# Halving the first and last quarter of the modulated input: two modulation vectors loaded, and w_in applied, in six parts instead of four

## Chip, cores and metric

One core of a Trainium2 chip. The metric is the device time of one execution in microseconds (us); of the kernel before, three runs gave a median of 1733.25 us (1733.23 to 1736.04).

## What is computed

A block of a streaming encoder over 256 positions of width 2048, in f32. What the change touches is its beginning:

```python
mod  = silu(c) @ w_ada + b_ada                  # six vectors of 2048
sh_m, sc_m, gt_m, sh_f, sc_f, gt_f = split(mod, 6)
h    = rms_norm(x, g_norm_mix) * (1 + sc_m) + sh_m
proj = h @ w_in          # 1024 columns of q and kv latent, 64 of rotary key, 3 x 1024 of the convolution
```

Then come the convolution and the attention on `proj`, `w_out`, a second modulated norm, and PEER: the 128 x 128 experts' scores against all keys, the best 16 per head, and the sum over the chosen rows of `peer_v`.

## The kernel before

Everything is held transposed: features on the 128 partitions, the 256 positions on the free axis, in 16 blocks of 128 features. A matrix product in f32 is made of three: each operand is split into a high and a low half (high = rounded copy by ScalarE, low = rest by VectorE, L198 and L199 for weights, L366 and L367 for h), and TensorE adds high x high, high x low and low x high (in column block 0 the low weights come second). A matmul of that kind has 128 x 128 weights and 256 columns.

The first two modulation vectors (m = 1, the scale, and m = 0, the shift) are made in quarters, 512 features each, by `ada_q(q)`. A quarter of a vector is 4 MB of `w_ada`, in four **chunks** of 1 MB (L407, buffers `t8`, six of them). Some chunks are multiplied by TensorE (L411: the activated c as weights in four column groups of 32, four matmuls of 512 columns a chunk, into `adarow`), by `ADA_PE` two of four for the scale and three of four for the shift; the rest by VectorE (L415, L417: four accumulating steps a chunk into `acc`). L420 adds both, the **column sums** (L423: four matmuls with one column) turn the row into columns, L316 adds the bias into `modc`. For the scale, L431 then makes x * rstd * (1 + scale) (`xs`); for the shift, `shift_split` makes the high and low half of h from it.

With a quarter of h the first 12 column blocks of `w_in` are worked on, in `unit`: 12 units, each of 4 feature blocks x 3 products = 12 matmuls (L694) into six PSUM tiles `pin` that stay open over all quarters. Their weights lie in `w_in0`, 12 tiles of 1 MB: three tiles per quarter, each with 4 column blocks x 4 feature blocks. A weight tile has a raw buffer (4 of them) and a high and a low buffer (2 of each), so the split of a tile waits until the tile two before it has been read.

Between the units the generator of the next quarter's modulation is advanced by the table `UNITS` (unit number: steps). A scheduler then orders the instructions of each engine; they run strictly in that order. All these loads are issued by the one queue of SyncE, in order. After each third of the last quarter's units, `after_in0` copies finished latent rows out (L681), and `lat_chain` squares and sums them (L474 to L480), takes the sum over features on TensorE (`ssl`, L341), the inverse root (L346 to L352, four small VectorE steps and a root on ScalarE) and spreads it by a matmul (`rlb`, L358). Then `conv_group` and `proj` go on with the other `w_in` tiles (`pwin`, L213, L214, L217).

Of the kernel before, what the change touches and what calls it, by code (L numbers as in the profile page):

```python
# [15 lines left out]
ALU = mybir.AluOpType  # L16
# [42 lines left out]
ADA_LAST = (0, 0, 1)  # L59
ADA_PE3 = (2, 5, 8, 11, 14)  # L60
PACES = {"start": 1.0, "latent": 1.15, "mixer": 1.35, "out": 0.83}
ADA_PE = {1: (1, 3), 0: (1, 2, 3)}
UNITS = {1: 1, 2: 1, 3: 1, 4: 1, 6: 1, 7: 1, 8: 2, 9: 1, 10: 1}
ABLK = 8
TB = 16

# [66 lines left out]
def hybrid_block_kernel(  # L133
# [22 lines left out]
    nc = tc.nc  # L156
# [81 lines left out]
    with tc.tile_pool(name="pre", bufs=1) as pre:  # L238
# [159 lines left out]
        xsv = {}  # L398

        def ada_q(q):  # L400
            for m in (1, 0):
                acc = s2(f"acc{m}_{q}")
                prow = ps_tile(f"adarow{m}_{q}")
                on_pe = ADA_PE[m]
                for kg in range(4):
                    raw = t8(f"ada{m}_{q}_{kg}", shape=(128, 4, 512))
                    nc.sync.dma_start(raw.rearrange("p a b -> p (a b)"), w_ada01[q, 1 - m, kg])  # L407
                    for j in range(4):
                        k = 4 * kg + j
# [12 lines left out]
                for j in range(4):  # L422
                    PE.matmul(prow[:, j:j + 1], lhsT=acc[:, j * 128:(j + 1) * 128], rhs=ones[:, 0:1],  # L423
                              start=True, stop=True)
                ada_cols(m, 4 * q, prow[:, :4])
                if m == 1:
                    xs = s2(f"xs{q}a"), s2(f"xs{q}b")
                    xsv[q] = [x_.rearrange("p (c t) -> p c t", c=2) for x_ in xs]
                    for j in range(4):
                        c = 4 * q + j  # L430
                        V.scalar_tensor_tensor(xsv[q][j // 2][:, j % 2], xt[:, c], modc[:, 1, c:c + 1], r0,  # L431
                                               ALU.mult, ALU.mult)
                yield

        def tiles():
# [252 lines left out]
        def unit(q, g, n, w):  # L688
            whi, wlo = w
            dst = pin[2 * g + n // 2][:, (n % 2) * 256:(n % 2) * 256 + 256]  # L690
            first = q == 0 and n % 2 == 0

            def one(j, wt, ht, start=False, stop=False):
                PE.matmul(dst, lhsT=wt[:, (4 * n + j) * 128:(4 * n + j + 1) * 128], rhs=ht[:, 4 * q + j],  # L694
                          start=start, stop=stop, skip_group_check=True)

            if g == 0 and n == 0:
                for j in range(4):
                    one(j, whi, h[0], first and j == 0)
                for j in range(4):  # L700
                    one(j, wlo, h[0])
                for j in range(4):
                    one(j, whi, h[1], False, q == 3 and j == 3)
                return
            for j in range(4):
                one(j, whi, h[0], first and j == 0)
                one(j, whi, h[1])
            for j in range(4):
                one(j, wlo, h[0], False, q == 3 and j == 3)

        def take0(i):
            return load_split(w_in0[i % NG0, i // NG0], f"win0_{i % NG0}_{i // NG0}", 0)

        for _ in ada_q(0):
            pass
        ws0 = {0: take0(0)}
        for q in range(4):
            nxt = ada_q(q + 1) if q < 3 else ada
            for j in range(4):
                c = 4 * q + j  # L720
                shift_split(xsv[q][j // 2][:, j % 2], modc[:, 0, c:c + 1], h[0][:, c], h[1][:, c])
            for u in range(4 * NG0):
                g, n = divmod(u, 4)
                i = NG0 * q + g
                if n == 0 and i + 1 < 4 * NG0:
                    ws0[i + 1] = take0(i + 1)
                unit(q, g, n, ws0[i])
                if q < 3:
                    for _ in range(UNITS.get(u, 0)):
                        next(nxt, None)  # L730
                elif n == 3:
                    after_in0(g)
                    for _ in range(ADA_LAST[g]):
                        next(nxt, None)
            if q == 0:
# [769 lines left out]
```

## Time and profile before

| | |
|---|---|
| median of three runs | 1733.25 us |
| the profiled execution | 1736.56 us, its span 1734.8 us |
| TensorE matmuls busy | 1671.4 us (96%) |
| VectorE busy | 1138.4 us (66%) |
| ScalarE busy | 704.6 us (41%) |
| DMA, mean over the span | 292 GB/s |

Spans and starts are in us from the start of the profiled execution. A granted clock of 1.00 is 2.4 GHz, 0.50 is 1.2 GHz. TensorE's matmuls overlap: a row's duration reaches to the modelled end, so the pace is read from the starts of consecutive rows. A matmul in f32 appears as two records (x8 for a chunk of four).

### The profile page before, as it was taken

The page shows a single profiled execution, that of the slowest core. Times are in us where ns is not written, and L with a number is a line of the kernel's source. Part 1 is how long each engine was busy: PE and PEld are TensorE (multiplying, and loading weights), DVE is VectorE, ACT ScalarE, POOL GpSimd, SP SyncE. Part 2 cuts the span into 40 slices and gives each one's busy share as a digit, 9 for nine tenths or more (in the row PEclk, how much of TensorE's full clock was granted, in tenths as well). Part 3 has the DMA queues.
Part 4 walks back from the last instruction along what each step waited for, and adds up shares of the span by engine and source line. Part 5 has one row for each costly group of instructions (what it writes and reads, how often), then busy time and mean ns, then how long its engine had stood idle before and what let it go on. Part 6 is the DMA issues. An engine that isn't in the chain of part 4 may idle for free. (4 is left out here: it accounts for less than half of the span.)

```text
span 1734.8 us, 30084 instructions
## 1 busy us (share of the span) xinstructions
PE 1671.4 (96%) x13011; PEld 1437.9 (83%) x13011; DVE 1138.4 (66%) x1481; ACT 704.6 (41%) x783; POOL 300.7 (17%) x257
## 2 busy tenths in 40 slices
PE   4999999999899999999999999999999999999996
PEld 2879899899899999999998999999999654444542
DVE  5778778767668989998985788765644332322324
ACT  3225557434544446645653343334343232222312
POOL 0000000000000000000001000000021486777771
PEclk9989999999999999999999999999999999999998
DMA  9987888878654456646678887879888699999895
GB/s 395 425 366 266 329 315 330 309 274 339 239 198 169 170 198 206 247 172 220 230 245 296 310 304 245 300 271 324 311 337 309 226 398 395 343 381 352 323 386 212
DMA packets 77928, 505.95 MB, mean 292 GB/s; under 512 B 9472, under 2 KB 10112, under 8 KB 22496
## 3 DMA queue, kind: packets, MB, share of 16 engines
q1 hardware_dynamic: 44784, 319.82, 49.1%
q0 software_dynamic: 29712, 162.94, 25.6%
q10 hardware_dynamic: 3296, 21.24, 3.2%
q8 instruction: 103, 1.69, 0.4%
q14 instruction: 33, 0.27, 0.0%
HBM read 466.21 MB, written 37.75 MB: 291 GB/s over the span
## 5 line engine op out<-in xcount | busy, mean ns | idle before, releaser
L213 PE MATMUL pu<-h2hi,hu 128*128 128x256 f32 x2048 | 495.3, 284 | 0.0
L198 ACT ACTIVATE hu<-ru 128x2048 fp32r<-128x2048 f32 x128 | 245.5, 1918 | 423.0 <-PE pu L214 382.6
L199 DVE TENSOR_TENSOR lu<-ru,hu 128x2048 fp32r<-128x2048 f32 x128 | 293.0, 2289 | 165.9 <-ACT hu L198 162.4
L213 PEld LDWEIGHTS pu<-h2hi,hu 128*128 128x128 f32 x2048 | 386.8, 189 | 0.2 <-issue 0.2
L217 PE MATMUL pu<-h2hi,lu 128*128 128x256 f32 x2048 | 264.5, 282 | 4.3 <-DVE lu L199 4.3
L217 PEld LDWEIGHTS pu<-h2hi,lu 128*128 128x128 f32 x2048 | 252.9, 190 | 4.5 <-DVE lu L199 4.5
L214 PE MATMUL pu<-h2loT3b,hu 128*128 128x256 f32 x1024 | 248.1, 281 | 0.0
L214 PE MATMUL pu<-h2loT3a,hu 128*128 128x256 f32 x1024 | 248.1, 281 | 0.0
L1293 PE MATMUL po<-rv,mc 128*64 128x512 f32 (+2 forms) x1064 | 221.7, 597 | 5.0 <-DMA mc<-actd,perm_idx 3.1
L214 PEld LDWEIGHTS pu<-h2loT3a,hu 128*128 128x128 f32 x1024 | 193.7, 189 | 0.2 <-issue 0.2
L214 PEld LDWEIGHTS pu<-h2loT3b,hu 128*128 128x128 f32 x1024 | 193.4, 189 | 0.0
L1293 PEld LDWEIGHTS po<-rv,mc 128*64 128x64 f32 (+2 forms) x1064 | 70.1, 130 | 145.5 <-issue 136.2
L1190 POOL DMA_DIRECT2D gg<-gd x16 | 18.8, 1172 | 905.3 <-DMA gd<-stage 905.3
L1242 POOL DMA_INDIRECT mc<-actd,perm_idx x109 | 134.8, 1237 | 36.8 <-issue 29.9
L1235 POOL DMA_INDIRECT rv<-in_peer_v_dram,perm_idx x107 | 129.2, 1207 | 61.5 <-issue 28.6
L204 DVE TENSOR_TENSOR lv<-rv,hv 128x2048 fp32r<-128x2048 f32 x24 | 55.0, 2293 | 115.4 <-ACT hv L203 115.3
L203 ACT ACTIVATE hv<-rv 128x2048 fp32r<-128x2048 f32 x24 | 45.9, 1914 | 123.4 <-DMA rv<-in_peer_v_dram,perm_idx 110.1
L199 DVE TENSOR_TENSOR lwin<-rwin,hwin 128x2048 fp32r<-128x2048 f32 x33 | 75.6, 2290 | 24.6 <-ACT hwin L198 24.5
L198 ACT ACTIVATE hwin<-rwin 128x2048 fp32r<-128x2048 f32 x33 | 63.1, 1913 | 61.0 <-PE pin L694 32.1
L204 DVE TENSOR_TENSOR third<-rv,third 128x2048 fp32r<-128x2048 f32 x12 | 27.6, 2296 | 89.4 <-ACT third L203 89.4
L1201 POOL DMA_DIRECT2D actd<-A x16 | 14.9, 934 | 407.0 <-DVE A L1196 224.3
L213 PE MATMUL pwin<-hhi,hwin 128*128 128x256 f32 x336 | 82.9, 289 | 0.0
(534 smaller groups left out, 2932.1 us busy)
## 6 DMA issues: line engine op xcount, KB each, us to landing
ru<-in_peer_u_dram SPq DMA_DIRECT2D x128, 1024.0 KB, 6.1
ada<-in_w_ada_dram SPq DMA_DIRECT2D x96, 1024.0 KB, 7.0
rwin<-in_w_in_dram SPq DMA_DIRECT2D x33, 1024.0 KB, 6.5
rwout<-in_w_out_dram SPq DMA_DIRECT2D x16, 1024.0 KB, 5.3
rwq<-in_w_q_dram SPq DMA_DIRECT2D x16, 1024.0 KB, 4.9
gd<-stage ACTq DMA_DIRECT2D x16, 1024.0 KB, 6.0
gg<-gd POOLq DMA_DIRECT2D x16, 1024.0 KB, 11.5
actd<-A POOLq DMA_DIRECT2D x15, 1024.0 KB, 6.3
```

Of the source, the lines that this page charges most:

```text
L198: S.activation(hi, raw, AF.Copy)
L199: V.tensor_tensor(lo, raw, hi.bitcast(F32), ALU.subtract)
L203: S.activation(hi, src, AF.Copy)
L204: V.tensor_tensor(lo, src, hi.bitcast(F32), ALU.subtract)
L213: PE.matmul(dst, lhsT=whi[:, sl], rhs=rhi[:, c], start=(c == sets[0][0]), stop=False)
L214: PE.matmul(dst, lhsT=whi[:, sl], rhs=rlo[:, c], start=False, stop=False)
L217: PE.matmul(dst, lhsT=wlo[:, sl], rhs=rhi[:, c], start=False, stop=(c == sets[-1][-1]))
L1190: keep(nc.gpsimd.dma_start(gg, gd[:, :, k * ABLK:(k + 1) * ABLK, :].rearrange("tb p i t -> p tb i t")))
L1201: keep(nc.gpsimd.dma_start(actd[k * ABLK * 128:(k * ABLK + n) * 128].rearrange("(i p) t -> p i t", p=128), ab[k][:, :n]))
L1235: keep(nc.gpsimd.indirect_dma_start(raw, None, v_rows, index(main[n])))
L1242: keep(nc.gpsimd.indirect_dma_start(ms[-1][:, n % 8], None, actd[:, :], index(main[n])))
L1293: keep(PE.matmul(po[tt * 4 + d4][row:row + size], lhsT=m[:, at * size:(at + 1) * size], rhs=raw[:, d4 * 512:(d4 + 1) * 512], start=start, ...
```

## The change

The first and the last quarter are each handled as two halves of 256 features, so that there are six parts: 0a, 0b, 1, 2, 3a, 3b. A half's modulation is made by `ada_half`: two chunks per vector, each with 8 feature blocks x 256 columns, and all of them go to TensorE, 8 matmuls of 256 columns a chunk; L455 masks the sum, and two column sums follow. Quarters 1 and 2 still use `ada_q`. The units of a half have 6 matmuls. In the halved quarters the three weight tiles are laid out anew: the first holds the first half's blocks 0 to 7, the second its blocks 8 to 11 and the second half's 0 to 3, the third the second half's 4 to 11.

```diff
-UNITS = {1: 1, 2: 1, 3: 1, 4: 1, 6: 1, 7: 1, 8: 2, 9: 1, 10: 1}
+UNITS = ({1: 1, 2: 1, 3: 1, 4: 1, 6: 1, 7: 1, 8: 2, 9: 1, 10: 1}, {1: 1, 3: 1, 4: 1, 6: 1, 8: 1, 9: 1})
+HALVED = (0, 3)
+PIECES = tuple((4 * q + 2 * k, 4 - 2 * (q in HALVED)) for q in range(4) for k in range(1 + (q in HALVED)))
+HALF0 = ([(0, n) for n in range(8)], [(0, n) for n in range(8, 12)] + [(1, n) for n in range(4)],
+         [(1, n) for n in range(4, 12)])
...
+        def ada_half(q, half):
+            for m in (1, 0):
+                prow = ps_tile(f"adarow{m}_{q}h{half}")
+                acc = s2(f"acc{m}_{q}h{half}")[:, :256]
+                for kg in range(2):
+                    raw = t8(f"ada{m}_{q}h{half}_{kg}", shape=(128, 8, 256))
+                    nc.sync.dma_start(raw.rearrange("p a b -> p (a b)"), w_ada01[q, 1 - m, 2 * half + kg])
+                    for j in range(8):
+                        k, r = 8 * kg + j, 32 * (j % 4)
+                        PE.matmul(prow[r:r + 32, :256], lhsT=cact[:, k:k + 1].to_broadcast([128, 32]), rhs=raw[:, j],
+                                  start=(k < 4), stop=(k >= 12), tile_position=(0, r))
+                    if kg == 0:
+                        yield
+                V.tensor_scalar(acc, prow[:, :256], quad, None, ALU.mult)
+                yield
+                for j in range(2):
+                    PE.matmul(prow[:, j:j + 1], lhsT=acc[:, j * 128:(j + 1) * 128], rhs=ones[:, 0:1],
+                              start=True, stop=True)
+                ada_cols(m, 4 * q + 2 * half, prow[:, :2])
+                if m == 1:
+                    scale_x(4 * q + 2 * half, 2)
                 yield
...
-        for q in range(4):
-            nxt = ada_q(q + 1) if q < 3 else ada
...
+        for q, (c0, size) in enumerate(PIECES):
+            nxt = ada_piece(q + 1) if q < end0 else ada
+            for c in range(c0, c0 + size):
+                shift_split(xsv[c // 2][:, c % 2], modc[:, 0, c:c + 1], h[0][:, c], h[1][:, c])
+            for u, (i, n, off) in enumerate(work0[q]):
+                if i + 1 < 4 * NG0 and i + 1 not in ws0:
                     ws0[i + 1] = take0(i + 1)
-                unit(q, g, n, ws0[i])
-                if q < 3:
-                    for _ in range(UNITS.get(u, 0)):
+                unit(n, range(c0, c0 + size), ws0[i], off, n == 0)
+                if q < end0:
+                    for _ in range(UNITS[PIECES[q + 1][1] == 2].get(u, 0)):
                         next(nxt, None)
```

On TensorE, at the border to quarter 1, the order was, with `adarow_1_420` the shift's row (the scale's, `adarow_1_303`, stands among the units well before):

```order
L694 MATMUL pin_181<-hhi,lwin_2_0_349 128x256 x2
L411 MATMUL adarow_1_420<-ada_1_3_469,cact 32x512 x4
L694 MATMUL pin_181<-hhi,lwin_2_0_349 128x256 x2
L423 MATMUL adarow_1_420<-ones,acc_1_419 128x1 x4
L694 MATMUL pin_176<-hhi,hwin_0_1_429 128x256
```

and of the change, where `adarow_1_413` is the scale's row and `adarow_1_494` the shift's, it is:

```order
L729 MATMUL pin_181<-hhi,lwin_2_0_352 128x256 x2
L415 MATMUL adarow_1_413<-ada_1_3_456,cact 32x512 x4
L427 MATMUL adarow_1_413<-ones,acc_1_412 128x1 x4
L415 MATMUL adarow_1_494<-ada_1_1_507,cact 32x512 x4
L415 MATMUL adarow_1_494<-ada_1_2_513,cact 32x512 x4
L415 MATMUL adarow_1_494<-ada_1_3_525,cact 32x512 x4
L427 MATMUL adarow_1_494<-ones,acc_1_493 128x1 x4
L729 MATMUL pin_176<-hhi,hwin_0_1_446 128x256
```

The scale's last chunk and its sums, and all of the shift's chunks, now stand between the units of part 0b and those of part 1.

On VectorE, at the end of the last part, the order before was (`lwin_1225` is the first weight tile behind the twelve, `rl0r` and `rl0v` the root's steps, `lacc` the sums of squares):

```order
L346 TENSOR_SCALAR rl0v<-ssl_1118 128x2
L199 TENSOR_TENSOR lwin_1225<-rwin_1222,hwin_1224 128x2048
L349 RECIPROCAL rl0r<-rl0r 128x2
L479 TENSOR_TENSOR lacc_1132<-lsq_1131 128x256
L350 SCALAR_TENSOR_TENSOR rl0v<-rl0v,rl0r 128x2
L500 TENSOR_TENSOR krT<-kraw,rope_t 128x256
L351 TENSOR_TENSOR rl0v<-rl0v,rl0r 128x2
L480 TENSOR_TENSOR lacc_1132<-lacc_1132 128x256
L352 SCALAR_TENSOR_TENSOR rl0r<-rl0v,rl0r 128x2
```

and of the change, where `lwin_1307` is the first weight tile behind the twelve and `lwin_1313` the second, it is:

```order
L203 TENSOR_TENSOR lwin_1307<-rwin_1304,hwin_1306 128x2048
L509 TENSOR_TENSOR lacc_1194<-lsq_1193 128x256
L507 TENSOR_TENSOR lacc_1238<-lsq_1237 128x256
L510 TENSOR_TENSOR lacc_1194<-lacc_1194 128x256
L530 TENSOR_TENSOR krT<-kraw,rope_t 128x256
L350 TENSOR_SCALAR rl0v<-ssl_1224 128x2
...
L203 TENSOR_TENSOR lwin_1313<-rwin_1310,hwin_1312 128x2048
L353 RECIPROCAL rl0r<-rl0r 128x2
...
L356 SCALAR_TENSOR_TENSOR rl0r<-rl0v,rl0r 128x2
```

The split that stands before the root's last steps is now that of the second tile, no longer that of the first. On TensorE the broadcast `rlb` that needs `rl0r` stands, in both, right behind the last unit and before the first matmul of `pwin`.

On TensorE the first units of part 0a read, in the change (`hwin_0_0` and `lwin_0_0` are the first tile's high and low half):

```order
L458 MATMUL adarow_0h_217<-ones,acc_0h_218 128x1 x2
L729 MATMUL pin_176<-hhi,hwin_0_0_245 128x256 x2
L729 MATMUL pin_176<-hhi,lwin_0_0_246 128x256 x2
L729 MATMUL pin_176<-hlo,hwin_0_0_245 128x256 x2
L729 MATMUL pin_176<-hhi,hwin_0_0_245 128x256
```

The low half of the weights is read by the third matmul; before, eleven matmuls stood ahead of the first one that reads it. On SyncE's queue the second and third weight tile of the last quarter (`rwin_1_3`, `rwin_2_3`), which followed the last modulation chunk, now stand before it. Behind this stage the order of every engine is the same as before but for a few neighbours that change places.

## Rows read from the trace of the kernel before

**Rows 1.** Busy time by stretches: engines' busy us, clock, DMA share, GB/s.
```profile
core 0: us, PE busy (x) PEld busy (x) DVE busy (x) ACT busy (x) POOL busy (x), PEclk, DMA share, GB/s
37.70:44.50 6.80, 4.88 (x23) 4.88 (x24) 5.49 (x6) 4.07 (x4) 0.00 (x0) 0.50 1.01 425
44.50:68.40 23.90, 22.67 (x180) 17.47 (x179) 16.46 (x24) 4.45 (x4) 0.00 (x0) 1.00 1.01 423
68.40:71.80 3.40, 3.40 (x16) 3.40 (x17) 2.08 (x5) 2.88 (x4) 0.00 (x0) 0.50 1.03 436
123.00:129.90 6.90, 6.11 (x29) 6.02 (x29) 4.14 (x6) 3.51 (x5) 0.00 (x0) 0.51 0.32 134
```

**Rows 2.** Timeline of TensorE (PE): start us, duration us, line, operation, count.
```profile
21.49 1.22 PE L358 MATMUL n0b<-ident,n0r 128*128 128x128 f32 x4 [3.55 <-DVE n0r L352]
22.64 3.64 PE L411 MATMUL adarow<-ada,cact 128*32 128x512 f32 x16
39.62 0.58 PE L694 MATMUL pin<-hhi,hwin 128*128 128x256 f32 x1 [3.39 <-ACT hwin L198]
47.67 1.06 PE L411 MATMUL adarow<-ada,cact 128*32 128x512 f32 x8
48.66 0.39 PE L694 MATMUL pin<-hhi,hwin 128*128 128x256 f32 x1
55.48 1.06 PE L411 MATMUL adarow<-ada,cact 128*32 128x512 f32 x8
57.42 1.05 PE L423 MATMUL adarow<-ones,acc 128*128 128x1 f32 x8
62.81 0.63 PE L694 MATMUL pin<-hhi,lwin 128*128 128x256 f32 x4
63.28 0.28 PE L694 MATMUL pin<-hhi,hwin 128*128 128x256 f32 x1
64.55 1.06 PE L411 MATMUL adarow<-ada,cact 128*32 128x512 f32 x8
66.49 1.05 PE L423 MATMUL adarow<-ones,acc 128*128 128x1 f32 x8 [0.44 <-DVE acc L420]
68.33 0.98 PE L694 MATMUL pin<-hhi,hwin 128*128 128x256 f32 x3 [0.80 <-ACT hhi L366]
95.87 1.01 PE L694 MATMUL pin<-hhi,hwin 128*128 128x256 f32 x3 [0.79 <-ACT hhi L366]
117.81 2.78 PE L411 MATMUL adarow<-ada,cact 128*32 128x512 f32 x24
144.18 0.61 PE L358 MATMUL rlb<-ident,rl0r 128*128 128x128 f32 x4
144.99 0.36 PE L213 MATMUL pwin<-hhi,hwin 128*128 128x256 f32 x1
```

**Rows 3.** Issues of modulation chunks, 105.4 to 105.6 us, with their time to landing.
```profile
L407 SPq DMA_DIRECT2D ada<-in_w_ada_dram x2: 327/371/415, 105.1 to 105.5; - x2
DMA to landing us min/median/max: 8.4/9.4/10.4
```

**Rows 4.** Waits of TensorE from 160 us to the end, longest group: total, times, longest.
```profile
PE pu L217 <- DVE lu L199: 4.3, 1, 4.3
```

**Rows 5.** Timeline of VectorE (DVE).
```profile
7.90 6.24 DVE L376 TENSOR_TENSOR sacc<-sacc,xsq 128x256 f32<-128x256 f32 x12
36.27 0.16 DVE L316 TENSOR_TENSOR modc<-adarow,vec 128x4 f32<-128x4 f32 x1 [1.14 <-PE adarow L423]
60.50 0.48 DVE L415 TENSOR_SCALAR acc<-ada,cact 128x512 f32<-128x512 f32 x1
61.01 2.33 DVE L417 SCALAR_TENSOR_TENSOR acc<-ada,cact,acc 128x512 f32<-128x512 f32 x3
139.74 2.29 DVE L199 TENSOR_TENSOR lwin<-rwin,hwin 128x2048 fp32r<-128x2048 f32 x1 [0.97 <-ACT hwin L198]
143.15 0.15 DVE L352 SCALAR_TENSOR_TENSOR rl0r<-rl0v,rl0r 128x2 f32<-128x2 f32 x1
```

**Rows 6.** Timeline of ScalarE (ACT), the weight split before the end of the stage.
```profile
137.79 1.92 ACT L198 ACTIVATE hwin<-rwin 128x2048 fp32r<-128x2048 f32 x1 [1.10 <-PE pin L694]
```

More of the change, by code (lines that the diff above doesn't have):

```diff
@@ L426, in ada_q, with scale_x @@
                 if m == 1:
[L427 to L432, printed above, removed]
+                    scale_x(4 * q, 4)
+                yield
+        def scale_x(c0, n):
+            for c in range(c0, c0 + n, 2):
+                x_ = s2(f"xs{c}")
+                xsv[c // 2] = x_.rearrange("p (c t) -> p c t", c=2)
+                for j in range(2):
+                    V.scalar_tensor_tensor(xsv[c // 2][:, j], xt[:, c + j], modc[:, 1, c + j:c + j + 1], r0,
+                                           ALU.mult, ALU.mult)
+        def ada_half(q, half):
[12 more added lines that the diff above has]
+                V.tensor_scalar(acc, prow[:, :256], quad, None, ALU.mult)
+                yield
+                for j in range(2):
+                    PE.matmul(prow[:, j:j + 1], lhsT=acc[:, j * 128:(j + 1) * 128], rhs=ones[:, 0:1],
[3 more added lines that the diff above has]
+                    scale_x(4 * q + 2 * half, 2)
                 yield
@@ L686, in after_in0, with unit @@
                 spawn(rope(krT, kraw[:, :256], "kr", kr_place))
-        def unit(q, g, n, w):
+        def unit(n, cs, w, off, tail=False):
             whi, wlo = w
[L690 to L709, printed above, removed]
+            dst = pin_nt(n)
+            first = cs[0] == 0 and n % 2 == 0
+            last = cs[-1] == 15
+            hh = [(whi, h[0], c) for c in cs]
+            hl = [(whi, h[1], c) for c in cs]
+            lh = [(wlo, h[0], c) for c in cs]
+            ops = hh + lh + hl if tail else [x for y in zip(hh, hl) for x in y] + lh
+            for k, (wt, ht, c) in enumerate(ops):
+                o = off + (c - cs[0]) * 128
+                PE.matmul(dst, lhsT=wt[:, o:o + 128], rhs=ht[:, c], start=first and k == 0,
+                          stop=last and k == len(ops) - 1, skip_group_check=True)
@@ L711, in take0, with ada_piece @@
         def take0(i):
             return load_split(w_in0[i % NG0, i // NG0], f"win0_{i % NG0}_{i // NG0}", 0)
-        for _ in ada_q(0):
+        def ada_piece(k):
+            q, half = divmod(PIECES[k][0], 4)
+            return ada_half(q, half // 2) if q in HALVED else ada_q(q)
+        work0 = []
+        for c0, size in PIECES:
+            q, half = divmod(c0, 4)
+            if q in HALVED:
+                work0.append([(NG0 * q + g, n, 256 * k) for g, us in enumerate(HALF0) for k, (p, n) in enumerate(us)
+                              if 2 * p == half])
+            else:
+                work0.append([(NG0 * q + n // 4, n, (n % 4) * 512) for n in range(4 * NG0)])
@@ L715, in hybrid_block_kernel @@
+        end0 = len(PIECES) - 1
+        for _ in ada_piece(0):
             pass
         ws0 = {0: take0(0)}
-        for q in range(4):
-            nxt = ada_q(q + 1) if q < 3 else ada
[L719 to L725, printed above, removed]
+        for q, (c0, size) in enumerate(PIECES):
[4 more added lines that the diff above has]
+                if i + 1 < 4 * NG0 and i + 1 not in ws0:
@@ L726, in hybrid_block_kernel @@
                     ws0[i + 1] = take0(i + 1)
-                unit(q, g, n, ws0[i])
-                if q < 3:
-                    for _ in range(UNITS.get(u, 0)):
+                unit(n, range(c0, c0 + size), ws0[i], off, n == 0)
+                if q < end0:
+                    for _ in range(UNITS[PIECES[q + 1][1] == 2].get(u, 0)):
                         next(nxt, None)
-                elif n == 3:
-                    after_in0(g)
-                    for _ in range(ADA_LAST[g]):
+                elif n % 4 == 3:
+                    after_in0(n // 4)
+                    for _ in range(ADA_LAST[n // 4]):
@@ L734, in hybrid_block_kernel @@
                         next(nxt, None)
+            if q < end0:
+                for _ in nxt:
+                    pass
             if q == 0:
@@ L1465 @@
     ada01 = np.ascontiguousarray(ada01).reshape(4, 2, 4, 128, 2048)
+    for q in HALVED:
+        part = w_ada[:, :, 1::-1, 512 * q:512 * q + 512].reshape(2, 8, 128, 2, 2, 256).transpose(3, 4, 0, 2, 1, 5)
+        ada01[q] = part.reshape(2, 4, 128, 2048)
     w_ada = w_ada[:, :, 2:].transpose(2, 0, 1, 3)
```

5 lines of the change are left out of this document (4 added, 1 removed).

## Prediction

> **What bounds the kernel now.** I read the busy time by stretches first, cut where the granted clock changes [rows 1]. In the stretch from 44.5 to 68.4 us two things are full at once: the DMA engines (share 1.01, 423 GB/s) and TensorE (22.67 of 23.90 us). Which of them ends the stage is told by TensorE's own order [rows 2]: a run of 4 unit matmuls takes 0.47 us (62.81 to 63.28), 0.1175 each, and 144 of them make 16.9 us. A loaded chunk of 1 MB on TensorE takes 1.0 us (47.67 to 48.66), and some 0.2 go at the two changes of form between it and the units around it (the matmul behind it takes 0.39, not 0.28): 1.2 us in the midst of units. A set of column sums is 1.05. From the first unit at 39.62 to the last, whose follower starts at 144.18, I count 576 x 0.1175 = 67.7 us of units, 15 chunks, 6 sets of column sums, gaps at the three borders between quarters, and stretches at the lower of the clock's two levels, 1.2 GHz instead of 2.4. Three of these stand in rows 1: 6.8 us from 37.7, 3.4 us from 68.4 and 6.9 us from 123; each begins at a gap before new units, and in the one of 3.4 us there is room for 16 matmuls where 29 would fit. So TensorE is the chain. The last modulation chunk is issued at 105.5 and lands 10.4 us later, at 115.9 [rows 3], but TensorE comes to its last chunks only at 117.81 [rows 2]. Data are ahead of TensorE by almost 2 us, and what counts is work and gaps on TensorE. After the stage its longest wait in all is 4.3 us [rows 4], so a shift passes on to the end.
>
> **The change part by part.** Names: parts 0a, 0b, 1, 2, 3a, 3b. I walk the changed order along TensorE; times are those of the profiled execution.
>
> *Start.* Now the squares are summed with accumulations of the first vector between them; without these, 15 additions at 0.52 (6.24 / 12) from 7.90 end at 15.7 [rows 5]. Some 1 us to VectorE and back, 0.2 for the root and four small operations of 0.2 (estimates from the root steps' rows) make 18.0, the broadcast 1.2 makes 19.2 [rows 2]. All four chunks of 0a have landed by then (4 MB behind x): half of today's eight. At the early rate (3.64 us for 2 chunks [rows 2]) the first vector is done at 22.8 and the second, with the first's column sums between (half of 1.05, at half the clock 1.05), at 27.5; accumulation 0.45, sums 1.05 and the addition make 29.2. Today that addition starts 3.35 us before the first unit (36.27 to 39.62 [rows 2, 5]); one split of 0.4 us less stands between: first unit at 32.1, which is 7.5 us earlier. But the new order takes the low weights third: they come 2.29 us [rows 5] after the high ones, so TensorE stops until 34.4. The early start is worth 5.2 us, not 7.5.
>
> *Part 0a.* 70 matmuls (8.2), three chunks (3.6), sums (0.5), and 2.4 us for a start at the lower clock as long as today's 4.9 us after 39.62: 49.1. Chunks of halves go to TensorE whole, 4 per part. Their 256-column form stands in no row. At its columns it costs the same 1.0 us per MB; at an unchanged time per matmul it costs 2.0, as there are twice as many. I take 1.0, since the nearest row, a unit matmul of 256 columns [rows 2], is paid by its columns (0.1175 at the higher level, twice that at the lower), and four column groups run side by side either way. The Trainium skill (TensorEngine Tiling, Instruction Overhead) puts about 60 cycles on each matmul; an estimate by it for the 8 added ones is 0.2 us a chunk, 2.4 us over the twelve after the start, 1751.4 in all.
>
> *Border 0a to 0b.* From the last chunk's start to the next first unit is 3.78 us today (64.55 to 68.33 [rows 2]). At half the columns the accumulation is some 0.33 shorter and the sums 0.5: 2.95, so 52.1. This border doesn't exist today, and it has the gap after which the clock falls: 1.7 us lost (half of 3.4).
>
> *Part 0b:* 8.5 + 1.2 + 1.7 = 11.4, so 63.5. *Border 0b to 1:* the order puts the last chunk and the sums of part 1's scale, and three chunks of its shift, behind all units of 0b; before, the scale was done under units. So VectorE's chain lies open: chunk to sums 1.94 (55.48 to 57.42), sums to the start of the shift's accumulation 3.08 (57.42 to 60.50), its four steps 2.8, the closing one 0.75, sums to first unit 1.84 (66.49 to 68.33) [rows 2, 5]. Part 1 starts at 73.9, against 68.33. The DMAs keep up: buffers come free later by as much as TensorE is late, and what it needs lands microseconds ahead.
>
> *Part 1* is as today, 27.54 us from first unit to first unit (68.33 to 95.87): 101.4. *Part 2:* 16.9, four chunks in its midst (4.8), two half sums (1.0), 1.7 for the clock, and the splits' 0.8 less the two matmuls above them: 25.0, so 126.4. *Part 3a:* 8.5 + 3.6 + 0.5 = 12.6, the border 2.95: 142.0. *Part 3b:* 8.5, and 1.7 for the clock: last unit at 152.2. Today that is 144.18, so the stage is **8.0 us longer**: 5.2 won at the start, 13 lost to seven chunks more on TensorE, their changes of form and two new borders. VectorE's saved accumulations (12 steps per halved quarter) gain nothing, for TensorE waited for them nowhere but at the borders.
>
> *What comes after 3b.* Today the last quarter has 20 us of units, under which the latent rows are copied out, squared and summed, and the inverse roots are ready when the units end: 144.18 to the next tile's first matmul at 144.99 [rows 2]. Part 3b has 10 us. And it meets the weight buffers: VectorE's order puts the low half of the second next tile ahead of the roots' last steps. That low half needs the high half, which waits for a buffer that the very last units read. Today the tile that is split there takes the buffer freed at two thirds of the quarter: high half at 137.79, low half at 139.74, root steps ended at 143.3 [rows 5, 6]. In the change, after the last unit: 1.92 + 2.29 + 1.1 for the steps = 5.3, while TensorE stands at the broadcast. ScalarE's copies, pressed together too, hold the sum of squares about 1 us (ends: 0 and 2). I take 6.3, and 1.7 for the clock after this gap (ends: 0 and 3.4). Queued behind are all matmuls of the projection. The price from below is 0, if these steps come in time.
>
> *Sum:* 8.0 + 6.3 + 1.7 = 16.0 us. The profiled execution took 1736.56, 3.3 more than the median; on it the change would take 1752.6, on the median of 1733.25 it takes **1749 us**.
>
> **Rivals.** (a) *The data end the stage.* If TensorE had room, its lateness would vanish and the last chunk decide. Two weight tiles now stand ahead of it in the queue that stood behind it; 2 MB at 423 GB/s are 5.0 us, so it lands at 120.9. Border 2.95, part 3b 10.2: last unit at 134.1, 10.1 earlier; less 5.3 to 8.0 for the wait behind it: 1728 to 1731, faster as long as that wait stays under 10. For it: the DMA share of 1.01. Against: matmuls that follow each other at 0.1175, and chunks taken 2 us after they landed. The weight loads are busy 17.47 of 23.90 us [rows 1], 73%. The Trainium skill (Perfetto Trace Analysis, Identifying the Most-Contended Engine) judges TensorE's headroom by that share and by MFU, not by matmul time; by that share a quarter of TensorE would be free and this rival would hold. Chance 0.10.
> (b) *The latent steps come in time* after 3b: the 8.0 us alone, 1741. For it: ScalarE and VectorE are not full there. Against: the order. 0.17.
> (c) *A 256-column matmul costs as much as one of 512:* 12 chunks at 1.0 more, 1761. 0.05.
> (d) *The clock stays up* at the new borders and at the start (2.4 + 1.7 + 1.7 less), and (b) too: 1735, no change that could be told. Against it: the border at 68.33, with 3.78 us from the last chunk to the unit, was followed by the lower level. 0.06.
> The forecast keeps 0.62.
>
> **Numbers.** 3.5 us (0.2%) is about what a measurement of this kernel can tell. The forecast, (b) and (c) are slower: 0.84; (d) the same: 0.06; (a) faster: 0.10. The forecast's own ends are 1743 (no clock loss at the new borders, none after 3b, no hold of the sums) and 1757 (three losses of twice the length and a hold of 2); with (b) on the lower side the range 1738 to 1757 holds about 0.79.
>
> **What would show it.** In the new profile: first unit at 32, a stop for low weights until 34; first units of 0b, 1, 2, 3a and 3b near 52, 74, 101, 126 and 142; the last unit at 152; a wait of about 5 us of TensorE's broadcast for the root steps, with a low-weight split before them on VectorE; chunks of 1.0 us each. The prediction is wrong if part 1 starts by 69, if the chunks wait for DMA, or if the projection's first matmul comes within 1 us of the last unit.

## Result and the profile after

The changed kernel takes 1747.41 us (median of four runs, 1744.18 to 1748.27), the kernel before in the same job 1733.24 (four runs, 1729.64 to 1736.04). The ratio is 1.0074, 95% interval 1.0059 to 1.0089: slower by 12.8 us (10.2 to 15.4); the two medians are 14.2 us apart. The forecast, 1749 us, was slower by 15.75: the direction is right, the time lies inside the range, and 15.75 stands just above the interval. The profiled execution of the change took 1748.27 us, its span 1745.6; against that of before (span 1734.8) only 10.8 us are left at the end, and where the other part went is one of the questions below.

TensorE's timeline of the changed kernel, at the points that the prediction named (columns as in [rows 2]):

```profile
29.37 0.80 PE L729 MATMUL pin<-hhi,hwin 128*128 128x256 f32 x2 [2.99 <-ACT hwin L202]
31.70 0.79 PE L729 MATMUL pin<-hhi,lwin 128*128 128x256 f32 x2 [1.53 <-DVE lwin L203]
48.88 0.97 PE L729 MATMUL pin<-hhi,hwin 128*128 128x256 f32 x3 [0.79 <-ACT hhi L370]
62.25 1.05 PE L427 MATMUL adarow<-ones,acc 128*128 128x1 f32 x8 [0.87 <-DVE acc L424]
63.23 2.78 PE L415 MATMUL adarow<-ada,cact 128*32 128x512 f32 x24
69.08 1.56 PE L427 MATMUL adarow<-ones,acc 128*128 128x1 f32 x8 [3.07 <-DVE acc L424]
71.44 0.79 PE L729 MATMUL pin<-hhi,hwin 128*128 128x256 f32 x2 [0.80 <-ACT hhi L370]
98.39 1.05 PE L427 MATMUL adarow<-ones,acc 128*128 128x1 f32 x8 [1.53 <-DVE acc L424]
100.24 1.01 PE L729 MATMUL pin<-hhi,hwin 128*128 128x256 f32 x3 [0.80 <-ACT hhi L370]
105.35 1.07 PE L451 MATMUL adarow_3h<-ada_3h,cact 128*32 128x256 f32 x16
106.35 0.39 PE L729 MATMUL pin<-hlo,hwin 128*128 128x256 f32 x1
125.15 0.86 PE L729 MATMUL pin<-hhi,hwin 128*128 128x256 f32 x5 [0.45 <-ACT hhi L370]
140.97 1.32 PE L729 MATMUL pin<-hhi,hwin 128*128 128x256 f32 x5 [0.79 <-ACT hhi L370]
151.03 0.58 PE L345 MATMUL ssl<-ones,lacc 128*128 128x1 f32 x4
151.67 0.40 PE L729 MATMUL pin<-hhi,lwin 128*128 128x256 f32 x2
157.10 1.19 PE L362 MATMUL rlb<-ident,rl0r 128*128 128x128 f32 x4 [5.04 <-DVE rl0r L356]
158.80 0.56 PE L217 MATMUL pwin<-hhi,hwin 128*128 128x256 f32 x1
```

The first units of 0a, 0b, 1, 2, 3a and 3b stand at 29.4, 48.9, 71.4, 100.2, 125.2 and 141.0 us. The first matmul of the units comes 10.2 us earlier than before, and TensorE soon stops for the low weights; part 1 is already 3.1 us late (71.44 against 68.33 in [rows 2]), after 3.07 us of waiting for VectorE's accumulation in the border from 0b. The halved chunk takes 1.00 us (105.35 to 106.35). The last unit's last matmul starts at 151.79, against 144.07 before: the stage is 7.7 us longer. In the whole stage the profile shows TensorE waiting for VectorE and ScalarE only, never for a DMA. Then the broadcast rlb, which had no wait before, waits 5.04 us, and the projection starts at 158.80, 13.8 us later than in [rows 2].

What VectorE and ScalarE do in that wait:

```profile
151.64 0.16 DVE L350 TENSOR_SCALAR rl0v<-ssl 128x2 f32<-128x2 f32 x1 [0.42 <-PE ssl L345]
153.81 2.29 DVE L203 TENSOR_TENSOR lwin<-rwin,hwin 128x2048 fp32r<-128x2048 f32 x1 [1.21 <-ACT hwin L202]
156.02 0.16 DVE L353 RECIPROCAL rl0r<-rl0r 128x2 f32<-128x2 f32 x1
156.80 0.16 DVE L356 SCALAR_TENSOR_TENSOR rl0r<-rl0v,rl0r 128x2 f32<-128x2 f32 x1
```

```profile
151.87 1.91 ACT L202 ACTIVATE hwin<-rwin 128x2048 fp32r<-128x2048 f32 x1 [0.66 <-PE pin L729]
153.69 0.19 ACT L352 ACTIVATE rl0r<-rl0v 128x2 f32<-128x2 f32 x1
```

The weight split on ScalarE waits for the last units' buffer (released by PE pin), the root stands behind it, the low half follows on VectorE, and the root's steps behind that. Before, the same split stood at 137.79 [rows 6] under units.

The granted clock by stretches (columns as in [rows 1]): the new gaps have stretches at the lower level, half the clock.

```profile
49.06:52.47 3.41, 3.41 (x17) 3.41 (x18) 3.30 (x6) 0.17 (x1) 0.00 (x0) 0.51 1.00 420
69.40:76.30 6.90, 6.10 (x30) 6.02 (x30) 3.74 (x6) 3.50 (x5) 0.00 (x0) 0.51 1.01 429
154.60:161.70 7.10, 4.60 (x22) 4.63 (x23) 5.79 (x15) 1.66 (x3) 0.00 (x0) 0.52 0.43 150
```

Up to 170 us TensorE spends 30.7 us at 1.2 GHz (in stretches that begin at 28.5, 49.0, 69.4, 100.2, 141.1 and 154.8), before 20.5.

From 164 to 313 us nearly everything is late by the same 15.06 us (around 211 a few neighbours have changed places). Then two parts of this come back. In the mixer the convolution's norm waits in the kernel before and not in the change. TensorE and VectorE before:

```profile
322.12 1.04 PE L358 MATMUL cn0b<-ident,cn0r 128*128 128x128 f32 x7 [2.59 <-DVE cn0r L352]
```

```profile
319.63 2.29 DVE L199 TENSOR_TENSOR lwin<-rwin,hwin 128x2048 fp32r<-128x2048 f32 x1 [2.34 <-ACT hwin L198]
321.91 0.16 DVE L352 SCALAR_TENSOR_TENSOR cn0r<-cn0v,cn0r 128x8 f32<-128x8 f32 x1
```

and VectorE after, where the two have changed places and TensorE does not wait:

```profile
333.32 0.17 DVE L356 SCALAR_TENSOR_TENSOR cn0r<-cn0v,cn0r 128x8 f32<-128x8 f32 x1
334.69 2.29 DVE L203 TENSOR_TENSOR lwin<-rwin,hwin 128x2048 fp32r<-128x2048 f32 x1 [1.21 <-ACT hwin L202]
```

This is the same fault as at 153.81, here in the kernel before: the lateness falls to 12.2 us. At the start of the query projection (pq) another 1.5 us come back, to 10.7, which stay to the end.

### The profile page after: what moved, and what is told of

The parts are those of the page before. It is cut to its first block, busy times and chain, and to the rows that moved or that the text cites. A ratio compares the mean times of both kernels' runs of the same rounds, so it can differ in the third digit from the quotient of the medians.

```text
span 1745.6 us, 30417 instructions
## 1 busy us (share of the span) xinstructions
PE 1679.4 (96%) x13182; PEld 1446.3 (83%) x13187; DVE 1126.0 (65%) x1467; ACT 704.2 (40%) x783; POOL 297.7 (17%) x257
## 5 line engine op out<-in xcount | busy, mean ns | idle before, releaser
L202 ACT ACTIVATE hu<-ru 128x2048 fp32r<-128x2048 f32 x128 | 245.5, 1918 | 423.6 <-PE pu L218 383.2
L203 DVE TENSOR_TENSOR lu<-ru,hu 128x2048 fp32r<-128x2048 f32 x128 | 293.0, 2289 | 166.0 <-ACT hu L202 165.0
L1276 POOL DMA_INDIRECT mc<-actd,perm_idx x109 | 138.3, 1268 | 36.9 <-issue 29.3
L1269 POOL DMA_INDIRECT rv<-in_peer_v_dram,perm_idx x107 | 122.8, 1148 | 64.0 <-issue 26.5
L203 DVE TENSOR_TENSOR lwin<-rwin,hwin 128x2048 fp32r<-128x2048 f32 x33 | 75.5, 2290 | 28.0 <-ACT hwin L202 26.0
L202 ACT ACTIVATE hwin<-rwin 128x2048 fp32r<-128x2048 f32 x33 | 63.0, 1912 | 63.7 <-PE pin L729 37.1
L208 DVE TENSOR_TENSOR third<-rv,third 128x2048 fp32r<-128x2048 f32 x12 | 27.5, 2292 | 85.7 <-ACT third L207 85.7
## 6 DMA issues: line engine op xcount, KB each, us to landing
gg<-gd POOLq DMA_DIRECT2D x16, 1024.0 KB, 11.3
```

The source lines that it names most:

```text
L202: S.activation(hi, raw, AF.Copy)
L203: V.tensor_tensor(lo, raw, hi.bitcast(F32), ALU.subtract)
L208: V.tensor_tensor(lo, src, hi.bitcast(F32), ALU.subtract)
L1269: keep(nc.gpsimd.indirect_dma_start(raw, None, v_rows, index(main[n])))
L1276: keep(nc.gpsimd.indirect_dma_start(ms[-1][:, n % 8], None, actd[:, :], index(main[n])))
```

## Experiments

Each ratio is to the kernel before on the same chip, with its 95% interval. Landmarks are TensorE starts in the profiled execution, "wait" is that of rlb; "last unit" is the start of its last matmul, "projection" is pwin's first matmul, "out" the output projection's, "experts" the first of pu. The code cuts are reduced to the lines that matter.

| kernel | ratio | first unit | part 1 | last unit | wait | projection | out | experts |
|---|---|---|---|---|---|---|---|---|
| before | 1 | 39.62 | 68.33 | 144.07 | 0 | 144.99 | 353.00 | 562.28 |
| changed | 1.0074 (1.0059 to 1.0089) | 29.37 | 71.44 | 151.79 | 5.04 | 158.80 | 365.20 | 572.99 |
| e1_first | 1.0045 (1.0025 to 1.0065) | 30.76 | 72.87 | 149.36 | 0 | 150.29 | 360.33 | 569.64 |
| e2_last | 1.0040 (1.0026 to 1.0053) | 38.10 | 66.45 | 145.24 | 5.04 | 152.25 | 357.88 | 565.74 |
| e3_roots | 1.0057 (1.0040 to 1.0074) | 29.50 | 71.57 | 152.26 | 1.34 | 154.76 | 361.47 | 570.79 |
| e4_cn0 | 0.9981 (0.9971 to 0.9991) | 39.36 | 67.87 | 143.46 | 0 | 144.38 | 351.18 | 561.12 |
| e5_chunks | 1.0013 (0.9998 to 1.0028) | 38.12 | 66.59 | 143.67 | 0 | 144.59 | 353.38 | 562.69 |
| e6_start | 1.0062 (1.0039 to 1.0086) | 28.31 | 69.88 | 150.52 | 5.04 | 157.53 | 363.19 | 572.48 |
| e7_share | 1.0100 (1.0076 to 1.0124) | 29.40 | 71.08 | 155.35 | 5.04 | 162.36 | 368.62 | 576.44 |
| e8_border | 1.0054 (1.0036 to 1.0072) | 30.39 | 70.91 | 150.53 | 5.04 | 157.55 | 363.09 | 570.96 |
| e9_both | 0.9982 (0.9962 to 1.0001) | 35.49 | 65.41 | 141.70 | 0 | 142.62 | 348.38 | 556.20 |
| e10_all | 1.0020 (1.0000 to 1.0040) | 27.48 | 67.18 | 147.66 | 1.34 | 150.16 | 355.25 | 564.50 |
| e11_first | 0.9975 (0.9954 to 0.9995) | 26.83 | 67.66 | 144.46 | 0 | 145.39 | 351.42 | 559.40 |

No edit touches what follows the experts' first matmul, yet from there to the end the thirteen profiled executions take between 1169.1 us (e6) and 1178.6 us (e2). So the landmarks of one execution show where time was won or lost, and the ratio, over all runs of a kernel, what came of it.

**Each half of the change alone.**

```diff
-HALVED = (0, 3)
+HALVED = (0,)      (e1_first)
+HALVED = (3,)      (e2_last)
```

> Only the first quarter is loaded in two halves; the last is whole, as before. Theory (the halves cost TensorE work and borders, and TensorE is the chain): first unit at 29 to 30 us, part 1 at 71 to 72 us against 68.33 before, so 3 us late in spite of the 10 us earlier start; from there the quarters as before, and after the last unit no wait for the root steps, since 20 us of units lie over them: the projection's first matmul at 148 to 150 us (144.99 before). The last root step of the convolution's norm stands behind the split of a weight tile on VectorE as in the kernel before, so the wait of 2.6 us there stays. Time: the kernel before plus 3 to 5 us, 1736 to 1738. Rival (the loss is the handover behind the last quarter alone, and the halved start is worth something): part 1 by 68.3, time 1733 or less.

> Only the last quarter is loaded in two halves; the first is whole, as before. Theory: first unit at 39.6 and part 1 at 68.3 us as before; from part 2's first unit to the last unit 51.5 us against 48.3 before (three more chunks on TensorE, one more border), so the last unit some 3 to 4.5 us late; then 5 us of wait for the root steps behind the low-half split, and 1 to 2 us of clock: the projection's first matmul 10 us late, at 155. Of this 2.6 to 2.9 us come back at the convolution's norm, whose last root step here stands ahead of the weight split. Time: the kernel before plus 6 to 8.5 us, 1739 to 1742. Rival (the two halves' losses feed each other, the last half alone has data in time): plus 3 or less.

The halved first quarter loses in spite of its start: part 1 at 72.87, last unit 5.3 us late, and the lateness passes to the projection unchanged, since rlb has no wait here. The place is as expected, the size is above it (ratio 1.0045, 7.8 us with an interval of 4.3 to 11.3, expected 3 to 5). Three things stand in its trace that the expectation did not have: the first unit comes 1.4 us later than in the changed kernel with the same start code, there is one more half-level stretch of 3.4 us, from 65.3, and the norm's wait, which this order keeps, is followed by another:

```profile
327.83 3.55 PE L362 MATMUL cn0b<-ident,cn0r 128*128 128x128 f32 x16 [2.59 <-DVE cn0r L356]
```

The halved last quarter behaves as expected in its lengths: from part 2's first unit (93.79) to the last unit 51.45 us, against 48.2 before (95.87 to 144.07), then the whole handover:

```profile
150.56 1.19 PE L362 MATMUL rlb<-ident,rl0r 128*128 128x128 f32 x4 [5.04 <-DVE rl0r L356]
```

Its landmarks lie 2 to 3 us ahead of the expected ones, since this execution already reached part 1 at 66.45 instead of 68.3. Its norm has the better order and no wait, and the time, 6.9 us more by the ratio, is as expected. The two ratios make 0.85% together, the whole change 0.74%: within the intervals the halves simply add.

**The handover.** (reduced; L202 and L203 stand in a helper)

```diff
-            S.activation(hi, raw, AF.Copy)
-            V.tensor_tensor(lo, raw, hi.bitcast(F32), ALU.subtract)
+            with tc.issue_after(root_of_rl0):
+                S.activation(hi, raw, AF.Copy)
+            with tc.issue_after(last_step_of_rl0):
+                V.tensor_tensor(lo, raw, hi.bitcast(F32), ALU.subtract)
```

> The changed kernel with both halves of the second next weight tile kept behind the latent root on ScalarE and behind its last step on VectorE. Theory (the 5.04 us wait of the broadcast is VectorE's and ScalarE's order, not their load): the last unit stays at 151.8 us, root steps done at 153 instead of 157, the wait of the broadcast 1 to 2 us, the projection's first matmul at 154 to 155 (158.80 in the changed kernel), and the second tile's low half, now at 156.5, still ahead of its use. Time: 4 to 5 us less than the changed kernel, 1742.5 to 1743.5. Rival (ScalarE and VectorE are full there): the split that is put off makes the next projection wait by as much, and the time stays at 1747.

```profile
153.88 0.68 PE L370 MATMUL rlb<-ident,rl0r 128*128 128x128 f32 x4 [1.34 <-DVE rl0r L364]
```

```profile
153.57 0.16 DVE L364 SCALAR_TENSOR_TENSOR rl0r<-rl0v,rl0r 128x2 f32<-128x2 f32 x1
156.63 2.29 DVE L209 TENSOR_TENSOR lwin<-rwin,hwin 128x2048 fp32r<-128x2048 f32 x1
```

The wait falls from 5.04 to 1.34 us and the projection starts 4.0 us earlier than in the changed kernel; at 313 us 3.7 are left. So the wait was an order and no lack of VectorE. By the ratios 2.9 us come through (1.0057 against 1.0074, with overlapping intervals), less than the 4 to 5 expected: in this execution the query projection does not give its 1.5 us back (see the last section).

**What was won back at the norm.** The same means on the kernel before, for the mixer's weight tile 19 behind the steps of cn0.

```diff
+PINNED = {"win19": "cn0"}
```

> The kernel before, with the split of one weight tile of the mixer kept behind the last root step of the convolution's norm on VectorE. Theory (what the changed kernel won back at 320 us is an order on VectorE that has nothing to do with halves): TensorE's wait of 2.59 us for that step at 322 is gone, everything after it 2.5 to 2.9 us earlier, time 1730.4 to 1731. Rival (the time passes into a later wait, of the query projection or the experts' stage): the gain shows at 322 and is gone by 480 us, time 1733.

```profile
320.30 2.05 PE L366 MATMUL cn0b<-ident,cn0r 128*128 128x128 f32 x16 [0.66 <-DVE cn0r L360]
```

The wait falls from 2.59 to 0.66, and TensorE goes from 0.1 us late to 1.8 early there, less than the 2.5 to 2.9 expected. The time is 0.9981 of before (0.9971 to 0.9991), 3.3 us: faster than both kernels, and nothing is halved. So most of what the change won at 320 us is an order that its different code happened to get; the kernel before can have it too. The trace keeps 1.2 us of it at the experts' start, so part of the median's gain is not explained by this place.

**The price of a chunk.** The kernel before, last quarter; its rows first, then those of the run.

```diff
-                on_pe = ADA_PE[m]
+                on_pe = (0, 1, 2, 3) if q == 3 else ADA_PE[m]
```

> The kernel before, no halves, with all eight chunks of the last quarter on TensorE instead of five. This prices a chunk alone. Theory (TensorE is the chain of the stage): three chunks at 1.0 us and 0.2 for the changes of form, so the last quarter's first unit at 127.5 us against 124.0, the last unit 3.0 to 3.6 us late, the projection's first matmul at 148 to 148.6; time 3 to 3.6 us more than the kernel before. Rival (the weight loads are busy only 73% of the stage, so TensorE has room and the data end it): the last quarter's first unit by 124.5, time as before.

```profile
122.13 1.09 PE L423 MATMUL adarow<-ones,acc 128*128 128x1 f32 x8 [1.53 <-DVE acc L420]
124.01 1.01 PE L694 MATMUL pin<-hhi,hwin 128*128 128x256 f32 x3 [0.79 <-ACT hhi L366]
```

```profile
94.00 1.01 PE L697 MATMUL pin<-hhi,hwin 128*128 128x256 f32 x3 [0.80 <-ACT hhi L366]
119.42 2.78 PE L411 MATMUL adarow<-ada,cact 128*32 128x512 f32 x24
123.07 1.05 PE L426 MATMUL adarow<-ones,acc 128*128 128x1 f32 x8 [0.88 <-DVE acc L421]
124.92 1.01 PE L697 MATMUL pin<-hhi,hwin 128*128 128x256 f32 x3 [0.80 <-ACT hhi L366]
```

From part 2's to the last quarter's first unit it takes 30.92 us, before 28.14 (95.87 to 124.01): 2.78 more, although the wait in front of the last sums fell by 0.65 (1.53 to 0.88). With that wait added back three chunks cost 3.43, 1.14 each: TensorE has no room. The time alone (1.0013, interval 0.9998 to 1.0028) could not have told this, and the expected places did not come: the last quarter's first unit stands at 124.92 instead of 127.5, the last unit at 143.67 instead of 3 us late. The execution's first unit is 1.5 us earlier than that of before with the same start code, and its last quarter has a half-level stretch of 3.4 us where before has 6.8.

**The stop at the start.** The first tile's weights are traced before the last column sums, and the first activations' split issued behind theirs.

```diff
+                with (tc.issue_after(highs["win0_0_0"]) if q == 0 else nullcontext()):
                     shift_split(xsv[c // 2][:, c % 2], modc[:, 0, c:c + 1], h[0][:, c], h[1][:, c])
```

> The changed kernel, with the first weight tile's split put ahead of the first split of the activations on ScalarE (the weights have landed at 22.0 us, ScalarE stands idle until 26.6 and splits them last). Theory (TensorE is the chain, the 1.5 us stop for the low weights is lost for good): first matmul of the first unit at 27.5 to 28 us (29.37), the run of units without a stop from 29.9 (31.70), part 1 at 69.6 (71.44), last unit 1.5 to 2 us earlier than in the changed kernel, and so the end: 0.9990 of its time. Rival (0a's own length is set by the chunks of 0b that land until 37.8): part 0b's first unit at 48.9 as now, no gain.

```profile
28.31 0.78 PE L731 MATMUL pin<-hhi,hwin 128*128 128x256 f32 x2 [0.79 <-ACT hhi L372]
29.98 0.50 PE L731 MATMUL pin<-hhi,lwin 128*128 128x256 f32 x2 [0.89 <-DVE lwin L205]
```

The units run from 29.98 instead of 31.70, part 1 stands at 69.88 (71.44) and the last unit is 1.3 us earlier: the stop is not made up by data that come later. The time, 1.0062, is lower by about 2 us as expected, but its interval (1.0039 to 1.0086) takes in the changed kernel's 1.0074.

**Chunks back to VectorE.** In 0b, 3a and 3b the first of the two chunks of each vector is accumulated on VectorE.

```diff
+                        if shared and kg == 0:
+                            V.scalar_tensor_tensor(acc, raw[:, j], cact[:, k:k + 1], acc, ALU.mult, ALU.add)
+                            continue
```

> The changed kernel, with one of the two chunks of each halved vector back on VectorE in 0b, 3a and 3b (six chunks fewer on TensorE; 0a as it is, since TensorE has nothing else to do there). Theory (the seven chunks more are the largest term of the longer stage): each chunk taken off gives 1.0 to 1.2 us, less what VectorE's eight steps of about 0.4 us add to a border; part 0b at 47 to 48 us, part 3a 2 us earlier against part 2's first unit, the last unit 3 to 7 us earlier than 151.8, time 3 to 7 us less than the changed kernel. Rival (VectorE's steps come to stand in the open borders, where TensorE waits for them): borders 2 to 3 us longer each, last unit unchanged or later.

```profile
142.73 1.01 PE L468 MATMUL adarow_3h<-ones,acc_3h 128*128 128x1 f32 x4 [6.29 <-DVE acc_3h L463]
```

```profile
136.47 3.61 DVE L456 SCALAR_TENSOR_TENSOR acc_3h<-ada_3h,cact,acc_3h 128x256 f32<-128x256 f32 x7
140.00 2.28 DVE L203 TENSOR_TENSOR lwin<-rwin,hwin 128x2048 fp32r<-128x2048 f32 x1
142.20 0.48 DVE L463 SCALAR_TENSOR_TENSOR acc_3h<-adarow_3h,quad,acc_3h 128x256 f32<-128x256 f32 x1
```

A miss, and the rival is right: the last unit is 3.6 us later than in the change, and the time is higher too (1.0100 against 1.0074, with overlapping intervals). The steps were taken at about 0.4 us and last 0.52 (3.61 / 7). The eight steps and a weight split come to stand before the closing accumulation, and TensorE waits 6.29 us in the border from 3a to 3b (0.61 in the change); in front of 0b it is 3.14. Only where units lie over the chunks is something won: part 2's first unit to 3a is 23.5 us (24.9). So in the middle of a part, under units, it paid to have the chunk on VectorE, and in front of a border to have it on TensorE.

**The border from 0b to 1.** One chunk more on TensorE, the second quarter's shift.

```diff
-                on_pe = ADA_PE[m]
+                on_pe = (0, 1, 2, 3) if (q, m) == (1, 0) else ADA_PE[m]
```

> The changed kernel, with the first chunk of the second quarter's shift on TensorE too (one chunk more there, 2.8 us of VectorE's steps less in the border from 0b to 1). Theory (that border is open to VectorE's chain, TensorE idle for 3.07 us before the sums at 69.08): the chunk costs 1.0 and the wait shrinks to 0.6 or less, part 1's first unit 1.5 to 2 us earlier at 69.5 to 70, the last unit and the end as much earlier. Rival (the last chunk's landing at 63.5 us sets the border): part 1 at 71.4 as now or later by the chunk.

```profile
69.06 1.05 PE L430 MATMUL adarow<-ones,acc 128*128 128x1 f32 x8 [0.86 <-DVE acc L425]
70.91 0.98 PE L732 MATMUL pin<-hhi,hwin 128*128 128x256 f32 x3 [0.79 <-ACT hhi L370]
```

The wait falls from 3.07 to 0.86. This execution reached 0b 1.3 us later than the changed kernel's (50.22) and part 1 still 0.5 earlier: 20.69 us between them against 22.56, so 1.9 won with a chunk more, as expected. Some 0.5 of it is the clock's: the sums ran at half of it in the change (1.56) and at full here (1.05). The time, 1.0054, is 3.5 us under the change's, with overlapping intervals.

**Everything together.** e9 is the kernel before with the orders of e4 and e6; e10 the change with those of e3, e6 and e8; e11 the halved first quarter with those of e4, e6 and e8.

```diff
+PINNED = {"win19": "cn0"}      (e9_both, e11_first)
+PINNED = {"win2": "rl0"}       (e10_all)
-HALVED = (0, 3)
+HALVED = (0,)                  (e11_first)
```

> The kernel before, no halves, with two orders changed: the weight split of the mixer behind the last root step of the convolution's norm (as in the run that did this alone), and the first weight tile's split ahead of the first activations on ScalarE (its weights land at 31.9 us, ScalarE is idle until 36.46). Theory (orders, not sizes, are what can be had here): first unit at 37.4 to 38 us against 39.62, no later stop, 1.5 to 2 us earlier from there to the end, and 1.8 to 2.8 more from 322 us: time 3.5 to 4.5 us less than the kernel before. Rival (the low weights then stop the first unit as in the changed kernel, or part 1's chunks set the pace): 2 to 3 less, as with the one order alone.

> The changed kernel, both quarters halved, with the three orders mended together: the first weight split early, the second quarter's shift all on TensorE, the second next weight tile behind the latent root. Theory (the terms add, as each sits on TensorE's chain): last unit 3 us earlier than 151.8, the projection's first matmul 7 us earlier, at 151.5 to 152; time 6 to 8 us less than the changed kernel, and still 5 to 8 us over the kernel before, which is what the chunks and the borders themselves cost. Rival (the terms cover each other): 3 to 4 us less than the changed kernel, as the best of them alone.

> Only the first quarter halved, with the first weight split early, the second quarter's shift all on TensorE, and the mixer's weight split behind the norm's last root step. Theory: of the 5.3 us by which the halved first quarter alone makes the last unit late, 3 come back, and 1.8 to 2.8 at the norm: time within 2 us of the kernel before, so the halved first quarter gains nothing over whole quarters with the same orders mended (the run of the kernel before with two orders). Rival (with the stops gone, the start that is 10 us earlier shows at last): the last unit before 144, time 3 us or more under the kernel before.

In e10 the terms do not cover each other: the last unit is 4.1 and the projection 8.6 us earlier than in the change, the time 9.4 us less (1.0020 against 1.0074), more than expected; it spends 20.5 us up to 170 at the lower level, 10 less than the change, which no single term had. It stays 3.5 us slower than the kernel before, with an interval that just reaches no change, where 5 to 8 were expected.

In e9 the first unit is at 35.49, better than expected, of which some 1.5 us are this execution's start (38.1 in e2 and e5, which have the start of before). It is 4.6 us ahead after the norm, as expected; the time, 0.9982 (0.9962 to 1.0001), agrees with that and does not exclude no change.

e11 is half a miss: its last unit stands at 144.46, 0.4 later than before and not earlier than 144, as the theory had it, so 4.9 of e1's 5.3 us came back and not 3 (e1's first unit was itself 1.4 late); it is 1.6 ahead after the norm. But its time, 0.9975 (0.9954 to 0.9995), is 4.3 us less than before, which is what the rival said. Which of e4, e9 and e11 is the fastest their overlapping intervals don't tell; e4 and e11 are faster than both kernels. That the halved first quarter wins by itself no run shows: after the norm e9, with whole quarters, is 3.0 us ahead of e11 (1.5 of them perhaps its execution's start), and in the profiled executions e11 gets ahead only behind the experts' start, where no edit reaches.

## Why the prediction came out as it did

**TensorE as the chain**: right. Chunks moved onto it cost 1.14 us each (e5) for a forecast of 1.2. Rival (a), by which the data end the stage, is refuted by the stage being 7.7 us longer, by TensorE never waiting for a DMA in it, and by e5. The Trainium skill (Perfetto Trace Analysis, Identifying the Most-Contended Engine) would by the weight loads' 73% have left a quarter of TensorE free; e5 disagrees, with 3.43 us for three chunks.

**A halved chunk at 1.0 us**: right, 1.00; the 2.0 of rival (c) is refuted. The 0.2 a chunk that was estimated from the Trainium skill (TensorEngine Tiling, Instruction Overhead) for the added matmuls are not seen either: 1.00 us for the halved chunk, 0.99 for the whole one in [rows 2].

**The start**: 2.7 us too late (29.4 for 32.1), for the 0a chunks were priced at the rate of half the clock, and in this execution the clock stood at the higher level from 21.7 us (before from 34.3). The terms up to the root add up to 17.7, not to the 18.0 that the prediction has; the trace has the broadcast at 18.14. The stop for the low weights was read rightly from the order, to 31.70 instead of 34.4.

**The stage by its parts** (forecast, measured): first unit to 0b 20.0, 19.5; 0b with its border to 1 21.8, 22.6; part 1 27.5, 28.8; part 2 25.0, 24.9; 3a with its border 15.6, 15.8; 3b to the last unit 10.2, 10.8. Part 1 was wrong by 1.3 because it was taken "as today". It is lost by the time VectorE closes the scale's row, before and after:

```profile
84.34 0.75 DVE L420 SCALAR_TENSOR_TENSOR acc<-adarow,quad,acc 128x512 f32<-128x512 f32 x1 [2.62 <-PE adarow L411]
```

```profile
88.74 0.75 DVE L424 SCALAR_TENSOR_TENSOR acc<-adarow,quad,acc 128x512 f32<-128x512 f32 x1 [3.93 <-PE adarow L415]
```

This is 17.3 us behind the part's first unit, before 16.0; from there to the next part it takes 11.5 us in both. Two things make it late, at some 0.7 us each (an estimate from the pace of the matmuls): the scale's second chunk stands behind 107 of the part's 144 unit matmuls on TensorE, before behind 101, and the half-level stretch covers the part's first 4.8 us, before 3.4.

The start was 2.7 us earlier than forecast and the parts together 2.3 longer (122.4 for 120.1). That the stage comes out at 7.7 for a forecast of 8.0 is luck to this extent: two misses nearly cancel.

**The handover**: right in place and cause; rival (b), by which the latent steps come in time, falls with the 5.04 us, and rival (d) with the half-level stretches at the new borders. From the last unit to the projection 7.0 us, before 0.9: 6.1 for 6.3. Here too one term stands in for another: the 1 us for a late sum of squares was not needed (ssl starts at 151.03, ahead of the last matmuls of the units), while the broadcast and the sums behind it ran at half the clock, 0.9 us more. The clock behind it cost 1.25 more, for 1.7. At 164 us the change was 15.06 late, for 16.0.

**The range**: the upper end of the forecast does not follow from its terms. Three losses of twice the length and a hold of 2 would make 1755.4 us, not 1757; the result lies below both.

**What failed** is the silent step that a shift "passes on to the end". 2.9 us came back at the norm, by an order on VectorE that the prediction had not read beyond the stage. It could have been read: the norm's wait of 2.59 stands in the profile of before, and the change's order was at hand. The forecast's 15.75 less 2.9 is 12.85; the ratio gives 12.8, though its interval leaves open anything from 10.2 to 15.4.

The other 1.5 us, at the query projection, could not have been read. With both quarters halved they came back in the changed kernel, e7 and e8, and not in e3, e6 and e10. The start moves between executions too: with the old start code the first unit stands at 39.62, 39.36, 38.10 and 38.12 (before, e4, e2, e5), with the new one at 29.37 to 30.76 (changed, e1, e3, e7, e8). So the 10.8 us between the two profiled spans are one pair of executions and not the price of the change. Which part of the medians' 14.2 us is the runs' spread no run shows.

## What to carry to other kernels

Halving a first and last load makes the first unit early, but it also halves the units that hide the next load's chain, the column sums and the buffers' turn; count the borders it adds before the microseconds of the start. Where a reshuffled kernel shows an engine waiting for four small steps, look whether a long split that waits for a buffer stands ahead of them in that engine's queue: here that order cost 5 us in one place and 2.6 in another, and 3.7 and 1.9 of these were won back without touching the sizes. Follow the order behind the change as far as the kernel goes, as its neighbours may move too.

## What the runs showed that was not expected

**A half-level stretch can be free.** From the query projection's first matmul to the first of the scores against the keys it takes 33.2 us before and 31.7 in the change. The split of its activations on VectorE holds its beginning; the longest such wait, before and after:

```profile
467.48 0.39 PE L214 MATMUL pq<-h2loT3a,hwq 128*128 128x256 f32 x1 [1.74 <-DVE h2loT3a L367]
```

```profile
479.67 0.39 PE L218 MATMUL pq<-h2loT3a,hwq 128*128 128x256 f32 x1 [0.16 <-DVE h2loT3a L371]
```

Before, the stretch at 1.2 GHz fell 6.5 us behind its start, where TensorE had begun to be the limit; in the change it covers the start, where VectorE is. The matmuls pq alone, first before, then after (columns as in [rows 1], without VectorE and GpSimd):

```profile
461.20:467.80 6.60, 4.20 (x28) 3.58 (x29) 0.00 (x0) 1.00 0.38 160
467.80:471.20 3.40, 3.40 (x18) 3.40 (x17) 0.00 (x0) 0.50 0.36 154
```

```profile
473.40:479.10 5.70, 5.59 (x24) 5.29 (x25) 0.00 (x0) 0.51 0.44 184
```

At full clock 28 matmuls were issued in 6.6 us with 2.4 us of waiting, at half the clock 24 in 5.7 with almost none. It goes with the place of the stretch in all thirteen profiled executions: 32.8 to 33.2 us in the seven where it begins 6.3 to 7.4 us behind pq's start (before, e1, e3, e4, e5, e6, e10), and 31.4 to 31.7 in the six where it covers that start. What sets the place was not tried.

**VectorE's steps don't halve with their columns.** An accumulating step on 128x256 takes 0.52 us (3.61 / 7 in e7), one on 128x512 0.78 (2.33 / 3 in [rows 5]). A chunk of 1 MB so costs VectorE 4 us in the halved form and 2.8 in the whole one, while on TensorE both take 1.0. This is one part of what made e7 a loss; the other is where its steps came to stand.
